# Where the first expert weights wait and in what pieces their places are filled again, in a decoder block on one core

## The chip, the cores and the metric

The kernel runs on one core of a Trainium2 chip. The metric is the device time of one execution in microseconds. Three runs of the kernel before gave 1254.2, 1250.68 and 1254.37 us, a median of 1254.2 us.

## The reference, cut to what matters

One decoder block over 256 tokens and 16 meta tokens, all float32. The first half normalises the stream, projects it, runs a pooling branch and a Mamba-2 branch, and merges them. The second half is a mixture of 64 experts in which each token uses two:

```python
def expert_block(args):
    xblk, e = args
    gu = xblk @ w_gu[e]                     # 1024 x 1024
    g, u = jnp.split(gu, 2, axis=-1)
    return (jax.nn.silu(g) * u) @ w_dn[e]   # 512 x 1024
...
y = yb * row_w[:, None].astype(yb.dtype)
out = jnp.zeros((T + 1, D), yb.dtype).at[row_tok].add(y)[:T]
```

The kernel reads the weights of all 64 experts, whatever the routing: 64 x (1024 x 1024 + 512 x 1024) x 4 bytes, which is 384 pieces of 1 MB (a MB is 1024 x 1024 bytes in this text, 1048.6 KB of the profile's GB/s).

## The kernel before, in words

**Rounds and items.** The experts go by in 16 rounds `q` of four. A round has 24 items of 1 MB, a tile of 128 x 2048 floats each: items 0 to 15 are gate and up weights, read by `up(q, xT)` at line 1094 in the order of `k` and `h`, and items 16 to 23 are down weights, read by `down` at line 1107. The items of all rounds are numbered through, so that item 24 is the first of round 1; the text calls them by these numbers (the item that the short description calls the 49th MB is 48). An item is worked on by eight matmul records on TensorE. Between `up` and `down` of a round TensorE gathers the next round's tokens (lines 978 and 969) and applies the gate (lines 993 to 1002).

**Where items lie.** Nearly all of SBUF outside the constants is one tile, `arena`, of 16 slots of 1 MB, in four blocks of four: block 0 holds the slots `r_w`, block 1 `s_rw` and `s_ce`, block 2 `s_yn` and `s_xs`, block 3 `s_bt`. During the first half it holds activations and the weights `wf`. Beside it there are `extra` (1 MB), `aux` (2 MB, used for items 11 and 12 and then for other things), rooms that the pools of the first half leave free (`mgA`, `mgB`, `ws...`), and, from the end of round 0, the tile `four` of 4 MB, which takes the place of those rooms.

**Who loads what.** Every weight load is issued by SyncE's queue (SP), in the order in which the program emits it. The first 25 items (`slots`, `load_e`, `load_1`, line 234) go one by one into places as the first half leaves them, between about 170 and 345 us. Then a load is emitted right behind the last use of the item whose place it takes: `used(m)` is called when the matmuls of item `m` have been emitted, and the load that it emits waits for them. Three kinds follow one another:

- `again` (line 261): items 25 to 39 go into places of the first 25, in pieces of one or two.
- `load_4` (line 248): from item 40, four items in one load of 4 MB, into one of five rooms (`rooms`: `four` and the blocks 3, 2, 0, 1), after the items in the list `frees`.
- line 251: the last eight items one by one.

The lists that set this are these:

```python
again = {0: (25, 1, s_xs[0]), 1: (26, 1, s_xs[1]), 4: (28, 2, two(a_bt)), ...}
frees = [23, 33, 35, 37, 39] + list(range(NS2 + 3, 16 * 24, 4))
```

An entry `m: (a, n, place)` says that after item `m` the `n` items from `a` are loaded into `place`. So in the kernel before item 23 frees the room for items 40 to 43, item 33 that for 44 to 47, item 35 that for 48 to 51, 37 and 39 those for 52 to 59, and from 43 on every fourth item frees one room.

A load on SP also waits until the eighth load before it has landed, since eight semaphores go round.

Of the kernel before, what the change touches and what calls it, by code (L numbers as in the profile page):

```python
# [9 lines left out]
FT = mybir.dt.float32  # L10
# [51 lines left out]
def block(ctx: ExitStack, tc: tile.TileContext, x, meta, csta_d, cstb_d, cstc_d, nfin_d, wf, gu_d, dn_d, out):  # L62
# [22 lines left out]
    extra = keep.tile([128, 2048], FT, name="extra")  # L85
    ACOLS = 32768
    ar = keep.tile([128, ACOLS], FT, name="arena")
# [5 lines left out]
    class Rot:  # L93
# [3 lines left out]
        def next(self):  # L97
# [6 lines left out]
    SLOT = 2048  # L104
    a_w = a
    a += NW * CHUNK
    a_row = a
# [4 lines left out]
    a_ce = a  # L112
# [6 lines left out]
    a_yn = a  # L119
# [10 lines left out]
    a_bt = a  # L130
# [30 lines left out]
    r_w = [ar[:, a_w + i * SLOT:a_w + (i + 1) * SLOT] for i in range(4)]  # L161
    s_xs, s_yn, s_rw, s_ce = [[ar[:, o + i * SLOT:o + (i + 1) * SLOT] for i in range(2)] for o in (a_xs, a_yn, a_row, a_ce)]
    s_bt = [ar[:, a_bt + i * SLOT:a_bt + (i + 1) * SLOT] for i in range(4)]
    WO0 = NSTEP - 8
    r_ws = [f"ws{(WO0 + k) % 4}" for k in range(4, 8)]
    slots = [s_xs[0], s_xs[1], s_rw[1], s_bt[0], s_bt[1], s_bt[3], s_rw[0], s_bt[2], r_w[0], s_yn[0], s_yn[1]]
    ONCE = len(slots)
    slots += [None, None, r_w[2], r_w[3], r_w[1], "mgA", r_ws[0], s_ce[0], s_ce[1], r_ws[1], "mgB", r_ws[2], r_ws[3], extra]
    NS = len(slots)
    assert NS == 25  # L170

    two = lambda o: ar[:, o:o + 2 * SLOT]
    again = {0: (25, 1, s_xs[0]), 1: (26, 1, s_xs[1]), 4: (28, 2, two(a_bt)), 6: (30, 2, two(a_row)), 7: (32, 2, two(a_bt + 2 * SLOT)),
             8: (27, 1, r_w[0]), 10: (34, 2, two(a_yn)), 14: (36, 2, two(a_w + 2 * SLOT)), 19: (38, 2, two(a_ce))}
    NS2 = NS + sum(n for _, n, _ in again.values())
    assert NS2 == 40
    slots += [None] * (NS2 - NS)
    for m_, n_, r_ in again.values():
        for j_ in range(n_):
            slots[m_ + j_] = r_[:, j_ * SLOT:(j_ + 1) * SLOT]  # L180

    rooms = [None] + [ar[:, i * 4 * SLOT:(i + 1) * 4 * SLOT] for i in (3, 2, 0, 1)]
    frees = [23, 33, 35, 37, 39] + list(range(NS2 + 3, 16 * 24, 4))

    def slot(m):
        return slots[m] if m < NS2 else part_of(rooms[(m - NS2) // 4 % 5], m % 4)
# [33 lines left out]
    n_e = [0]  # L220
    PER = 24

    def src_of(m, n=1):

        q, i = divmod(m, PER)
        v = gu_d[q, i // 4] if i < 16 else dn_d[q, (i - 16) // 4]
        return v[:, (m % 4) * SLOT:(m % 4 + n) * SLOT]

    def load_1(m):

        if isinstance(slots[m], str):
            pool = wsp if slots[m].startswith("ws") else mgp
            slots[m] = pool.tile([128, SLOT], FT, name="room" + slots[m], tag=slots[m], bufs=1)
        nc.sync.dma_start(out=slot(m), in_=src_of(m))

    def load_e():
        load_1(n_e[0])
        n_e[0] += 1

    n_4 = [NS2]  # L240
# [1 line left out]
    def load_4():  # L242
        m = n_4[0]
        n_4[0] += 4
        if m >= 16 * PER:
            return
        if m < 16 * PER - 8:
            nc.sync.dma_start(out=rooms[(m - NS2) // 4 % 5], in_=src_of(m, 4))
        else:
            for j in range(4):  # L250
                nc.sync.dma_start(out=slot(m + j), in_=src_of(m + j))

    def used(m):

        if m == 23:
            right.close()
            p = ctx.enter_context(tc.tile_pool(name="four", bufs=1, side="right", reuse_waits="tile"))
            rooms[0] = p.tile([128, 4 * SLOT], FT, name="four")
        if m in again:
            a_, n_, r_ = again[m]  # L260
            nc.sync.dma_start(out=r_, in_=src_of(a_, n_))
        if m in frees:
            load_4()
# [93 lines left out]
    for src, n, i in ((xm, NM, 2), (xh[:, 0, :], 128, 0), (xh[:, 1, :], 128, 1)):  # L357
        a_, b_ = slice(0, 512), slice(512, 1024)
# [353 lines left out]
    for n_ in (46, 46, 46, 57, 58, 68, 74, 80, 81, 82, 88):  # L712
        at(n_, load_e)
# [21 lines left out]
    n = NPROJ  # L735
# [60 lines left out]
    for k in range(8):  # L796
        wh, wl = get_piece(n)
        n += 1
        if k < 6:
            merge(k + 2)  # L800
        for _ in range((3, 0, 1, 0, 0, 0, 0, 0)[k]):
            load_e()
        W_[k] = wh, wl
        for kk, t in (((k, 0), (k, 1)), (), ((6, 0), (7, 0), (6, 1), (7, 1)))[0 if k < 6 else k - 5]:
            mh, ml = mgh[kk][:, t * 128:(t + 1) * 128], mgl[kk][:, t * 128:(t + 1) * 128]
            wh, wl = W_[kk]
            for lw, rw, f, l in ((mh, wh, True, False), (mh, wl, False, False), (ml, wh, False, True)):
                for h in range(2):
                    T.matmul(wo[2 * t + h], lw, rw[:, h * 512:(h + 1) * 512], start=kk == 0 and f, stop=kk == 7 and l,
                             skip_group_check=True)  # L810
        if k == 3:
            load_1(16)
        for _ in range((0, 0, 0, 0, 2, 3, 0, 0)[k]):
            load_e()
            if n_e[0] == 16:
                n_e[0] += 1
# [271 lines left out]
    def up(q, xT):  # L1088
        pg, pu = bank(mps, "pg", 1), bank(mps, "pu", 1)
        for k in range(8):  # L1090
            for h, ps in ((0, pg), (1, pu)):
                w = slot(q * PER + 2 * k + h)
                for e in range(4):
                    T.matmul(ps[32 * e:32 * e + 32], xT[:, k, 32 * e:32 * e + 32], w[:, e * 512:(e + 1) * 512],  # L1094
                             start=k == 0, stop=k == 7, skip_group_check=True)
                used(q * PER + 2 * k + h)
                if q == 15 and (k, h) == (5, 1):
                    keep_warm("gx", 12)
        return pg, pu

    def down(q, after):
        for hf in range(2):
            py = bank(mps, ("pg", "pu")[hf], 1)
            for c in range(4):
                w = slot(q * PER + 16 + 4 * hf + c)
                for e in range(4):
                    T.matmul(py[32 * e:32 * e + 32], hsT[:, c, 32 * e:32 * e + 32], w[:, e * 512:(e + 1) * 512],  # L1107
                             start=c == 0, stop=c == 3, skip_group_check=True)
                used(q * PER + 16 + 4 * hf + c)
                if q == 15 and (hf, c) in WARM:  # L1110
                    keep_warm("gx", WARM[hf, c])
            combine(py, hf, q == 0, q == 15)
            after(hf)
# [163 lines left out]
```

## Time and profile before

| | us |
|---|---|
| median of three runs | 1254.2 |
| the profiled execution | 1250.28 |
| its span, first to last instruction | 1248.7 |
| TensorE busy in the span | 969.6 |
| VectorE, ScalarE, GpSimd busy | 322.8, 293.2, 142.6 |
| packets of SP's queue (q1) | 459.94 MB (10^6 bytes), 88.2% of 16 DMA engines' span |

The page gives, for 40 equal slices of the span, the busy share of each engine, the granted TensorE clock, the mean busy share of the core's 16 DMA engines and what they moved. The chain of waits follows the work back from the last instruction; 43% of it is DMA and 40% TensorE. The first half of the block ends at about 340 us, round 0 at about 394 us and round 1 at about 434 us.

### The profile page before, as it was taken

How to read it: one execution, taken by the hardware profiler on the slowest of the kernel's cores; microseconds unless marked ns; L12 is line 12 of the kernel's file. 1: busy time of each engine (PE TensorE's matmuls, PEld its weight loads, DVE VectorE, ACT ScalarE, POOL GpSimd, SP SyncE). 2: the span in 40 equal slices, each digit the busy share in tenths (PEclk: the TensorE clock that was granted, in tenths of full speed). 3: DMA queues.
4: the chain of work that ended last, by engine and by line, in shares of the span. 5: the costliest groups of instructions: out<-in, count | busy, mean ns of one | idle time of the engine just before them, and what ended most of it. 6: DMA issues, size and time to landing. Idle time of an engine off the chain costs nothing.

```text
span 1248.7 us, 15306 instructions
## 1 busy us (share of the span) xinstructions
PE 969.6 (78%) x6621; PEld 542.6 (43%) x6621; DVE 322.8 (26%) x545; ACT 293.2 (23%) x561; POOL 142.6 (11%) x118
## 2 busy tenths in 40 slices
PE   9999999999988767676776657675568676776666
PEld 9999999899852312222221212131213222121222
DVE  6899987777721000000000000000000000000001
ACT  7887656633320101001010101010101001010102
POOL 2334444344100000000000000000000000000000
PEclk9999999999998978787878888797968787878889
DMA  7544447667998999999999999999999999999996
GB/s 291 185 156 168 169 171 268 254 252 270 376 403 367 419 431 428 433 436 432 431 430 435 435 430 430 434 434 431 431 433 434 433 428 435 434 431 431 432 427 253
DMA packets 27847, 462.04 MB, mean 370 GB/s; under 512 B 3112, under 2 KB 3440, under 8 KB 5504
## 3 DMA queue, kind: packets, MB, share of 16 engines
q1 hardware_dynamic: 27408, 459.94, 88.2%
q8 instruction: 53, 0.87, 0.3%
q10 hardware_dynamic: 368, 1.08, 0.2%
q14 instruction: 18, 0.15, 0.0%
HBM read 459.93 MB, written 1.08 MB: 369 GB/s over the span
## 4 chain that ended last, share of the span: by engine, by line
DMA 43%; PE 40%; DVE 9%; ACT 6%; issue 2%; POOL 0%; ACTq 0%; DVEq 0%; SPq 0%; POOLq 0%
DMA arena<-gu 32%; PE pg L1107 7%; DMA four<-gu 5%; PE gx L978 5%; PE pg L1094 4%; PE pu L1094 4%; DMA arena<-dn 3%; DVE whl L305 3%; ACT xT L969 3%; PE pj L328 2%; PE pj L322 2%; PE pj L324 2%; PE pj L323 2%; DMA four<-dn 2%; DVE arena L498 1%
## 5 line engine op out<-in xcount | busy, mean ns | idle before, releaser
L1094 PE MATMUL pg<-arena,xT 128*32 128x512 f32 x816 | 145.0, 791 | 123.0 <-DMA arena<-gu 123.0
L1008 DVE COPY aux<-tr 128x256 f32<-128x256 f32 x16 | 6.8, 424 | 687.4 <-PE tr L1007 687.4
L969 ACT ACTIVATE xT<-gx,csta 128x128 f32<-128x128 f32 x124 | 35.3, 367 | 526.5 <-PE gx L978 518.8
L1094 PE MATMUL pu<-arena,xT 128*32 128x512 f32 x824 | 134.7, 732 | 0.0
L305 DVE TENSOR_TENSOR whl<-arena,whl 128x1024 fp32r<-128x1024 f32 x79 | 115.3, 1462 | 26.4 <-ACT whl L304 25.8
L1094 PEld LDWEIGHTS pg<-arena,xT 128*32 128x32 f32 x816 | 27.1, 134 | 213.5 <-DMA arena<-gu 144.8
L322 PE MATMUL pj<-hn,whl 128*128 128x272 f32 (+1 forms) x384 | 113.6, 296 | 0.0
L324 PE MATMUL pj<-hn,whl 128*128 128x272 f32 (+1 forms) x384 | 109.7, 286 | 0.4 <-DVE whl L305 0.4
L323 PE MATMUL pj<-hn,whl 128*128 128x272 f32 (+1 forms) x384 | 109.5, 285 | 0.1
L1024 POOL TENSOR_TENSOR aux<-sel,wte 128x128 f32<-128x128 f32 x32 | 12.1, 399 | 831.1 <-DVE sel L921 786.8
L304 ACT ACTIVATE whl<-arena 128x1024 fp32r<-128x1024 f32 x86 | 90.5, 1057 | 52.0 <-PE so L324 28.9
L978 PE MATMUL gx<-sel,xh 128*128 128x128 f32 x480 | 61.5, 281 | 29.2 <-ACT xT L969 18.6
L1020 PE MATMUL acc<-aux 128*128 128x512 f32 x128 | 63.5, 618 | 24.1 <-ACT aux L1018 23.2
L1107 PE MATMUL pg<-arena,aux 128*32 128x512 f32 x400 | 69.2, 852 | 9.6 <-ACT aux L1002 7.1
L322 PEld LDWEIGHTS pj<-hn,whl 128*128 128x128 f32 x384 | 72.4, 188 | 2.5 <-issue 1.5
L323 PEld LDWEIGHTS pj<-hn,whl 128*128 128x128 f32 x384 | 72.6, 189 | 1.2 <-issue 1.2
L1094 PEld LDWEIGHTS pu<-arena,xT 128*32 128x32 f32 x824 | 32.7, 137 | 92.5 <-issue 92.5
L324 PEld LDWEIGHTS pj<-hn,whl 128*128 128x128 f32 x384 | 72.3, 188 | 0.6 <-DVE whl L305 0.6
L978 PEld LDWEIGHTS gx<-sel,xh 128*128 128x128 f32 x480 | 55.8, 192 | 36.2 <-ACT xT L969 21.4
L1094 PE MATMUL pg<-four,xT 128*32 128x512 f32 x192 | 37.2, 859 | 38.6 <-DMA four<-gu 38.6
L305 POOL TENSOR_TENSOR whl<-arena,whl 128x1024 fp32r<-128x1024 f32 x19 | 48.5, 2555 | 69.0 <-ACT whl L304 69.0
L1020 PEld LDWEIGHTS acc<-aux 128*128 128x128 f32 x128 | 21.7, 189 | 69.3 <-ACT aux L1018 52.3
(351 smaller groups left out, 1324.6 us busy)
## 6 DMA issues: line engine op xcount, KB each, us to landing
arena<-gu SPq DMA_DIRECT2D x44, 4096.0 KB, 42.4
arena<-dn SPq DMA_DIRECT2D x23, 4096.0 KB, 41.4
arena<-wf SPq DMA_DIRECT2D x48, 1024.0 KB, 5.0
four<-gu SPq DMA_DIRECT2D x12, 4096.0 KB, 42.8
four<-dn SPq DMA_DIRECT2D x5, 4096.0 KB, 38.0
arena<-gu SPq DMA_DIRECT2D x17, 1024.0 KB, 7.5
arena<-gu SPq DMA_DIRECT2D x6, 2048.0 KB, 17.7
arena<-dn SPq DMA_DIRECT2D x6, 1024.0 KB, 34.4
```

Source lines behind the costliest of these rows:

```text
L304: S.activation(wh, w, AF.Copy)
L305: (G if n in on_pool else V).tensor_tensor(out=wl, in0=w, in1=wh.bitcast(FT), op=OP.subtract)
L322: T.matmul(ps, wh, ah, start=start, stop=False, skip_group_check=True)
L323: T.matmul(ps, wh, al, start=False, stop=False, skip_group_check=True)
L324: T.matmul(ps, wl, ah, start=False, stop=stop, skip_group_check=True)
L328: T.matmul(ps.rearrange("p (i n) -> p i n", n=NT), wh, a, start=start, stop=False, skip_group_check=True)
L498: V.scalar_tensor_tensor(out=acc[:, j:], in0=ps[:, :NA - j], scalar=cs("cw", ct * 4 + 3 - j), in1=acc[:, j:], op0=OP.mult, op1=OP.add)
L969: S.activation(xT[:, 4 * b + k, :], ps[:, k * 128:(k + 1) * 128], AF.Copy, scale=cs("nf", 4 * b + k))
L978: T.matmul(ps[:, k * 128:(k + 1) * 128], xh[:, t, (4 * b + k) * 128:(4 * b + k + 1) * 128], sel[:, t, :], start=t == 0, stop=t == 1, skip_ ...
L1020: T.matmul(acc[t][h], ctv[:, t * 128:(t + 1) * 128], yv, start=first, stop=last, skip_group_check=True)
L1094: T.matmul(ps[32 * e:32 * e + 32], xT[:, k, 32 * e:32 * e + 32], w[:, e * 512:(e + 1) * 512], start=k == 0, stop=k == 7, skip_group_check= ...
L1107: T.matmul(py[32 * e:32 * e + 32], hsT[:, c, 32 * e:32 * e + 32], w[:, e * 512:(e + 1) * 512], start=c == 0, stop=c == 3, skip_group_check ...
```

## The change

The order in which the places are filled before round 0 stays, place by place (the new list `order`), but the items that lie in them change: items 0 to 3 lie in block 3, 4 to 7 in block 2, 8 and 9 in half of block 1, and 10, 13, 14 and 15 in block 0. So items that are used one behind the other share a block. The second pass (`again`) now covers items 25 to 47 instead of 25 to 39, in pieces of one to four, and rooms of 4 MB (`load_4`) begin with item 48 instead of 40.

| after item | loads, before | loads, after |
|---|---|---|
| 0 to 5 | 25; 26; 28 and 29 (after 4) | 25; 26; 27; 28; 29; 32, one each |
| 6 to 10 | 30, 31; 32, 33; 27; 34, 35 | 30, 31 (after 7); 34, 35 (after 9) |
| 14, 15 | 36, 37 (after 14) | 36 to 39 (after 15) |
| 18, 19 | 38, 39 (after 19) | 33; 40 |
| 23 | 40 to 43 | 41 to 43 |
| 24, 25, 27 | nothing | 44; 45; 46, 47 |
| 32, 33, 35, 37 | 44 to 47 (33); 48 to 51 (35); 52 to 55 (37) | 48 to 51 (32) |
| 39, 40 | 56 to 59 (39) | 52 to 55 (39); 56 to 59 (40) |
| 43, 47, ... | 60 to 63; 64 to 67; ... | the same |

```diff
-    slots = [s_xs[0], s_xs[1], s_rw[1], s_bt[0], s_bt[1], s_bt[3], s_rw[0], s_bt[2], r_w[0], s_yn[0], s_yn[1]]
+    slots = s_bt + s_xs + s_yn + s_rw + [r_w[0]]
...
+    order = [4, 5, 9, 0, 1, 3, 8, 2, 10, 6, 7] + list(range(11, 24))
...
-    again = {0: (25, 1, s_xs[0]), 1: (26, 1, s_xs[1]), 4: (28, 2, two(a_bt)), 6: (30, 2, two(a_row)), 7: (32, 2, two(a_bt + 2 * SLOT)),
-             8: (27, 1, r_w[0]), 10: (34, 2, two(a_yn)), 14: (36, 2, two(a_w + 2 * SLOT)), 19: (38, 2, two(a_ce))}
+    again = {0: (25, 1, s_bt[0]), 1: (26, 1, s_bt[1]), 2: (27, 1, s_bt[2]), 3: (28, 1, s_bt[3]), 4: (29, 1, s_xs[0]), 5: (32, 1, s_xs[1]),
+             7: (30, 2, two(a_yn)), 9: (34, 2, two(a_row)), 15: (36, 4, ar[:, a_w:a_w + 4 * SLOT]), 18: (33, 1, s_ce[0]), 19: (40, 1, s_ce[1]),
+             23: (41, 3, None), 24: (44, 1, extra), 25: (45, 1, s_bt[0]), 27: (46, 2, two(a_bt + SLOT))}
...
-    rooms = [None] + [ar[:, i * 4 * SLOT:(i + 1) * 4 * SLOT] for i in (3, 2, 0, 1)]
-    frees = [23, 33, 35, 37, 39] + list(range(NS2 + 3, 16 * 24, 4))
+    rooms = [ar[:, i * 4 * SLOT:(i + 1) * 4 * SLOT] if i < 4 else None for i in (2, 0, 1, 4, 3)]
+    frees = [32, 39, 40, 43, 47] + list(range(NS2 + 3, 16 * 24, 4))
...
     def load_e():
-        load_1(n_e[0])
+        load_1(order[n_e[0]])
         n_e[0] += 1
...
-            rooms[0] = p.tile([128, 4 * SLOT], FT, name="four")
+            rooms[3] = p.tile([128, 4 * SLOT], FT, name="four")
         if m in again:
             a_, n_, r_ = again[m]
+            if r_ is None:
+                r_ = rooms[3][:, 0:n_ * SLOT]
+                place(a_, n_, r_)
             nc.sync.dma_start(out=r_, in_=src_of(a_, n_))
```

On SP's queue the rows up to the last load of the first pass (`room<-dn`) are the same in both kernels but for line numbers. Behind it stands, in the kernel before (a row of 128x2048 is 1 MB, 128x4096 two, 128x8192 four; L261 is the second pass, L248 the rooms of 4 MB):

```order
L234 DMA room<-dn 128x2048
L261 DMA arena<-gu 128x2048 x2
L261 DMA arena<-gu 128x4096 x3
L261 DMA arena<-gu 128x2048
L261 DMA arena<-gu 128x4096 x3
L248 DMA four<-dn 128x8192
L248 DMA arena<-dn 128x8192
L248 DMA arena<-gu 128x8192 x3
L248 DMA four<-gu 128x8192
```

and in the kernel after (L272 is the second pass, L256 the rooms of 4 MB):

```order
L242 DMA room<-dn 128x2048
L272 DMA arena<-gu 128x2048 x6
L272 DMA arena<-gu 128x4096 x2
L272 DMA arena<-gu 128x8192
L272 DMA arena<-gu 128x2048
L272 DMA arena<-dn 128x2048
L272 DMA four<-dn 128x6144
L272 DMA extra<-dn 128x2048
L272 DMA arena<-dn 128x2048
L272 DMA arena<-dn 128x4096
L256 DMA arena<-gu 128x8192 x3
L256 DMA four<-gu 128x8192
```

Items 25 to 47 are carried by 15 loads instead of 11; the single load of 44 to 47 that stood behind `four<-dn` has become three loads into `extra` and two places of block 3. From item 48 on every load is one of 4 MB in both.

On TensorE the only rows that differ say where `down(1)` and the rounds behind it read their weights. Before:

```order
L999 MATMUL tr<-ident,aux 128x128 x4
L1107 MATMUL pg<-four,aux 32x512 x16
L1020 MATMUL acc_3821<-aux 128x512
L1020 MATMUL acc_3823<-aux 128x512
L1107 MATMUL pu<-arena,aux 32x512 x16
```

After:

```order
L1010 MATMUL tr<-ident,aux 128x128 x4
L1118 MATMUL pg<-arena,aux 32x512 x4
L1118 MATMUL pg<-four,aux 32x512 x12
L1031 MATMUL acc_3821<-aux 128x512
L1031 MATMUL acc_3823<-aux 128x512
L1118 MATMUL pu<-extra,aux 32x512 x4
L1118 MATMUL pu<-arena,aux 32x512 x12
```

Item 40 now lies in `arena`, items 41 to 43 in `four`, 44 in `extra` and 45 to 47 in `arena`; the number and the order of the matmuls are unchanged. The rows of VectorE, ScalarE and GpSimd are the same.

## Rows read from the trace of the kernel before

**Rows 1.** The page's 40 slices of 31.2 us each: clock, DMA share, GB/s.

```profile
PEclk9999999999998978787878888797968787878889
DMA  7544447667998999999999999999999999999996
GB/s 291 185 156 168 169 171 268 254 252 270 376 403 367 419 431 428 433 436 432 431 430 435 435 430 430 434 434 431 431 433 434 433 428 435 434 431 431 432 427 253
```

**Rows 2.** Windows by stage: bounds, length, busy per engine (count), clock, DMA share, GB/s.

```profile
core 0: us, PE busy (x) PEld busy (x) DVE busy (x) ACT busy (x) POOL busy (x), PEclk, DMA share, GB/s
352.00:356.00 4.00, 4.00 (x44) 1.24 (x40) 0.00 (x0) 3.90 (x15) 0.00 (x0) 1.00 0.78 236
356.00:392.00 36.00, 27.85 (x205) 11.65 (x198) 4.93 (x22) 6.22 (x14) 2.12 (x7) 0.91 1.03 432
392.00:400.00 8.00, 7.11 (x46) 2.95 (x48) 2.20 (x13) 0.00 (x0) 0.00 (x0) 0.79 0.94 399
400.00:410.00 10.00, 10.00 (x100) 3.09 (x96) 0.00 (x0) 0.00 (x0) 0.00 (x0) 1.00 0.52 195
410.00:450.00 40.00, 26.62 (x202) 10.47 (x194) 1.73 (x5) 4.65 (x12) 0.76 (x2) 0.96 1.01 434
450.00:1180.00 730.00, 500.53 (x3054) 171.36 (x3050) 22.52 (x65) 60.53 (x156) 9.87 (x26) 0.82 1.00 432
1230.00:1238.00 8.00, 6.86 (x48) 2.79 (x49) 1.38 (x2) 1.37 (x4) 0.00 (x0) 1.00 0.46 189
```

**Rows 3.** SP's queue in order of time, 378 to 445 us: start, length, line, load.

```profile
383.80 0.33 SPq L261 DMA_DIRECT2D arena<-gu  x1
390.07 0.33 SPq L248 DMA_DIRECT2D four<-dn  x1
405.79 0.33 SPq L248 DMA_DIRECT2D arena<-dn  x1
407.51 3.76 SPq L248 DMA_DIRECT2D arena<-gu  x3
424.94 0.33 SPq L248 DMA_DIRECT2D four<-gu  x1
431.27 6.66 SPq L248 DMA_DIRECT2D arena<-dn  x2
```

**Rows 4.** Windows of 2 us from 400 to 408 us, columns as in rows 2.

```profile
400.00:402.00 2.00, 2.00 (x24) 0.62 (x20) 0.00 (x0) 0.00 (x0) 0.00 (x0) 1.00 0.68 270
402.00:404.00 2.00, 2.00 (x24) 0.65 (x20) 0.00 (x0) 0.00 (x0) 0.00 (x0) 1.00 0.15 66
404.00:406.00 2.00, 2.00 (x26) 0.54 (x20) 0.00 (x0) 0.00 (x0) 0.00 (x0) 1.00 0.00 0
406.00:408.00 2.00, 2.00 (x24) 0.63 (x20) 0.00 (x0) 0.00 (x0) 0.00 (x0) 1.00 0.91 262
```

**Rows 5.** Chain of waits, 394 to 462 us: start, length, what ended last.

```profile
395.31 1.84 PE pg L1094 x8
397.15 1.71 PE pu L1094 x8
398.86 0.86 PE pg L1094 x8
399.72 0.86 PE pu L1094 x8
...
404.01 0.86 PE pg L1094 x8
404.87 0.86 PE pu L1094 x8
...
410.02 0.86 PE pu L1094 x8
...
421.24 3.69 PE pg L1107 x32
...
424.94 33.05 DMA four<-gu
```

**Rows 6.** Loads issued at 364.6, 390.1 and 405.8 us: count, KB, us to landing.

```profile
arena<-gu SPq DMA_DIRECT2D x1, 2048.0 KB, 23.9
...
four<-dn SPq DMA_DIRECT2D x1, 4096.0 KB, 15.1
...
arena<-dn SPq DMA_DIRECT2D x1, 4096.0 KB, 12.1
```

**Rows 7.** A stretch of loads of 1 MB alone, columns as in rows 2.

```profile
340.00:350.00 10.00, 10.00 (x87) 9.62 (x86) 7.08 (x37) 2.93 (x8) 0.00 (x0) 1.00 1.01 423
```

**Rows 8.** Chain of waits at the end, from 1175 us.

```profile
1175.54 6.08 PE pg L1107 x32
...
1181.64 35.74 DMA arena<-gu
...
1217.44 20.05 DMA four<-dn
...
1237.54 1.11 PE pu L1107 x8
```

More of the change, by code (lines that the diff above doesn't have):

```diff
@@ L170, in block, with place @@
     assert NS == 25
+    order = [4, 5, 9, 0, 1, 3, 8, 2, 10, 6, 7] + list(range(11, 24))
     two = lambda o: ar[:, o:o + 2 * SLOT]
-    again = {0: (25, 1, s_xs[0]), 1: (26, 1, s_xs[1]), 4: (28, 2, two(a_bt)), 6: (30, 2, two(a_row)), 7: (32, 2, two(a_bt + 2 * SLOT)),
-             8: (27, 1, r_w[0]), 10: (34, 2, two(a_yn)), 14: (36, 2, two(a_w + 2 * SLOT)), 19: (38, 2, two(a_ce))}
+    again = {0: (25, 1, s_bt[0]), 1: (26, 1, s_bt[1]), 2: (27, 1, s_bt[2]), 3: (28, 1, s_bt[3]), 4: (29, 1, s_xs[0]), 5: (32, 1, s_xs[1]),
+             7: (30, 2, two(a_yn)), 9: (34, 2, two(a_row)), 15: (36, 4, ar[:, a_w:a_w + 4 * SLOT]), 18: (33, 1, s_ce[0]), 19: (40, 1, s_ce[1]),
+             23: (41, 3, None), 24: (44, 1, extra), 25: (45, 1, s_bt[0]), 27: (46, 2, two(a_bt + SLOT))}
     NS2 = NS + sum(n for _, n, _ in again.values())
-    assert NS2 == 40
+    assert NS2 == 48
     slots += [None] * (NS2 - NS)
+    def place(m, n, r):
+        for j in range(n):
+            slots[m + j] = r[:, j * SLOT:(j + 1) * SLOT]
     for m_, n_, r_ in again.values():
-        for j_ in range(n_):
-            slots[m_ + j_] = r_[:, j_ * SLOT:(j_ + 1) * SLOT]
-    rooms = [None] + [ar[:, i * 4 * SLOT:(i + 1) * 4 * SLOT] for i in (3, 2, 0, 1)]
-    frees = [23, 33, 35, 37, 39] + list(range(NS2 + 3, 16 * 24, 4))
+        if r_ is not None:
+            place(m_, n_, r_)
+    rooms = [ar[:, i * 4 * SLOT:(i + 1) * 4 * SLOT] if i < 4 else None for i in (2, 0, 1, 4, 3)]
+    frees = [32, 39, 40, 43, 47] + list(range(NS2 + 3, 16 * 24, 4))
     def slot(m):
```

## The prediction

> **What bounds the kernel now.** I read the page's slices first [rows 1]. From the eleventh slice on, that is from about 320 us, the 16 DMA engines are busy all the time at about 432 GB/s, with one slice below its neighbours: the thirteenth, 375 to 406 us, with 367 GB/s. Behind it TensorE's clock falls again and again, because TensorE waits. The windows by stage make this exact [rows 2]: from 450 to 1180 us the share is 1.00 at 432 GB/s while TensorE works in 500.53 of 730 us. The rounds are bound by the weights' transfer, and TensorE has room for some 30% more. So the end comes when the last weight has landed, and only two things move it: the bytes, which the change leaves alone, and the time in which the DMA engines have nothing to carry.
>
> The same windows show that time. From 352 to 356 us there are 236 GB/s, from 392 to 400 us 399, from 400 to 410 us only 195, and both neighbours of that stretch run at 432 and 434. SP's queue tells why [rows 3]: after the load at 390.07 us (items 40 to 43) the next one leaves at 405.79 us. In the windows of 2 us the share is 0.68, 0.15 and 0.00 before it, and 0.91 after it [rows 4]. What the load at 405.79 waits for stands in the chain of waits [rows 5]: round 1's `up` starts at 395.31 us, its first two items take 1.84 and 1.71 us and the others 0.86, and its tenth item, item 33, ends at 404.87 + 0.86 = 405.73 us. Item 33 is what frees the room for 44 to 47. TensorE is at work all the time there; the queue is empty because no room is free by the kernel's lists. Further on the chain is a wait for a load of 4 MB, 33.05 us long, and so it goes to the end [rows 5, 8].
>
> **The change, part by part.** *The first items.* The places are filled at the same times and in the same order; only which item lies in each changes. The last of these loads leave before 350 us, and until then the first half sets the pace. The items that come later in the new order of places (6 and 7 instead of 9 and 10) are loaded well before `up(0)`, which starts at about 350 us. I cost this at nothing; what hides it is the first half's work on TensorE, which is busy for 10.00 of 10 us from 340 to 350 [rows 7].
>
> *The second pass up to item 23.* Items 0 to 5 free one place each instead of 0, 1 and 4. The first two loads leave as before, so the dip at 352 to 356 us stays. By item 19, 16 MB are out instead of 15. Before, the 15th MB was nearly carried when `four<-dn` left at 390.07: the share of 392 to 400 us, 399 GB/s against 432, is worth 8 x 33 / 432 = 0.6 us. One MB takes 1.0486 / 432 = 2.43 us, so the 16th keeps the engines busy until about 394 us and I expect this to go too.
>
> *Items 44 to 47.* This is the core. Nineteen MB are out by 390 us in both kernels and are carried by about 401 to 402 us [rows 4]. In the new lists item 24 releases 44, item 25 releases 45 and item 27 releases 46 and 47: by the chain these leave at 397.15, 398.86 and about 400.6 us [rows 5]. The first of them is more than 4 us ahead of the empty queue, and the load into the empty queue at 405.79 was moving bytes within the next window [rows 4], so 4 us are enough. Four more MB last 9.7 us, until about 411. Item 32 (ends at 404.87) releases 48 to 51, which last until 421; item 39 (ends at 410.88) releases 52 to 55, until 431; item 40, the first of `down(1)`, ends at 421.24 + 3.69 / 4 = 422.2 and releases 56 to 59; and 60 to 63 leave at 424.94 as before. Each release stands 9 us or more ahead of the moment at which the queue would run dry. Nothing is late next: what was a hole is filled through to the steady rounds, whose lists are the same.
>
> *New waits.* Item 33 now stands behind 36 to 39 in the queue. It is the 15th MB, so it lands by about 393 us and is read at 404.87. The new loads wait for the eighth load before them; with pieces of 1 MB that one is some 10 MB older and has landed. Four more loads on SP cost four issues of 0.33 us each [rows 3] on a queue that sits idle for tens of us: nothing.
>
> *The size of the hole.* Over all 16 engines it is (432 - 195) / 432 x 10 = 5.5 us from 400 to 410, and with the 0.6 us above 6.1 us: the upper end. But a load has landed only when its slowest engine is through. The load at 364.6 us landed at 364.6 + 23.9 = 388.5, that of 390.07 at 405.2, that of 405.79 at 417.9 [rows 6]. From 388.5 to 417.9 there landed 2 + 4 + 4 = 10 MB, 24.3 us of work in 29.4 us: 5.1 us lost for the last engine. From 405.2 to 417.9 alone it is 12.7 - 9.7 = 3.0 us, the lower end, if the engine that lagged at 405 would have lagged on. I take 5.1, since it is measured on landings over the whole hole.
>
> *Smaller pieces.* Ten loads of 1 MB take the place of three. In a stretch of 1-MB loads alone the engines move 423 GB/s [rows 7], which is 2.48 instead of 2.43 us per MB: 7 x 0.05 = 0.4 us lost. [...]
>
> **Sum.** 5.1 - 0.4 = 4.7 us. Against the profiled execution (span 1248.7, with 1.58 us around it 1250.28) that is 1245.6 us. This execution and one of the three runs lie 3.5 to 3.9 us below the median of 1254.2; from the median the same sum gives 1249.5 us, which I predict.
>
> **Rivals.**
>
> *The slowest DMA engine sets the gain.* The engines do not finish together: at the end, where the queue runs dry, the share over 1230 to 1238 us is only 0.46, and at 402 to 404 it is 0.15 while the load that it belongs to lands at 405.2 [rows 2, 4, 6]. In the kernel before, the hole lets an engine that lags catch up, since all start again together; with the hole filled, the lag of 3 us at 405 stays and adds to what gathers until 1237. Then the gain is 3.0 - 0.4 = 2.6 us and the time 1251.6. For it speaks the slope of the drain; against it, that the lag need not fall on the engines that are last at the end.
>
> *Starts that add up: slower.* A load that comes into an empty queue took 12.1 us for what takes 9.7 in a full one [rows 6]: 2.4 us of start. If the four additional loads each paid it, 9.6 us would be lost and 5.1 won, 1254.2 + 4.5 = 1258.7 us. It decides as soon as the queue holds nothing behind the load in work, which could happen between 397 and 405 us if `up(1)` started later than now. Against it stand the 423 GB/s of the 1-MB loads [rows 7] and the lead of 4 us. [...]
>
> *The hole only moves: no change.* Were `up(1)` to wait for item 33, or `down(1)` for 40, the later rooms would come free later, and the same 5 us would lie between 411 and 425 us: 1254.2. The margins of 9 us above speak against it.
>
> **How the numbers follow.** The forecast has a chance of 0.70, the slowest engine 0.16, the hole that moves 0.08, the added starts 0.06. A measurement of this kernel can tell about 0.3%, 3.8 us, from no change. The forecast lies only 0.9 us beyond that, and runs of the same kernel lie up to 3.7 us apart, so of its 0.70 I count 0.58 as faster and 0.12 as the same. The slowest engine gives 0.04 faster, 0.11 same, 0.01 slower; the hole that moves 0.07 same and 0.01 slower; the added starts 0.01 same and 0.05 slower. Together 0.62 faster, 0.31 same, 0.07 slower. The range begins at the upper end of the hole taken from the faster runs, 1250.28 - 6.1 = 1244.2, and reaches to no gain at all, 1254.5; the forecast's own range is 1244.2 to 1251.6.
>
> **What would show it.** In the changed kernel's profile: loads on SP at about 397, 399 and 400.6 us; a DMA share near 1.00 and over 420 GB/s in every window between 392 and 450 us; the load of 60 to 63 landing near 453 us instead of 458; the same 432 GB/s from 450 us on; the last weight landing some 5 us before 1237.5 us and the same 11 us from there to the end [rows 8]. A share below 0.9 between 405 and 430 us would mean that the hole has moved; a full share there with less than 3 us won at the end, that the slowest engine sets it; and a lower rate in the stretch of small loads, that starts add up. A different rate in the steady rounds would prove the whole sum wrong, since 730 us at 432 GB/s weigh far more than the hole.

## The result, and the profile after

| | before | after |
|---|---|---|
| median of the first measurement (5 runs each), us | 1254.14 | 1243.56 |
| its ratio, with the 95% interval | | 0.9939 [0.9921, 0.9956] |
| median of a later session on one chip (29 and 6 runs), us | 1250.46 | 1243.60 |
| its ratio | | 0.9952 [0.9936, 0.9968] |
| the profiled execution, us | 1250.28 | 1243.56 |

The kernel became faster. The forecast was 1249.5 us with a range from 1244.2 to 1254.5; the time lies 0.6 us below that range. Three of the five runs of before in the first measurement lie between 1254.1 and 1254.4 us; of the 81 runs of before in the three sessions below 8 lie near 1254 (1253.9 to 1254.6), and the others between 1246.9 and 1252.1. So the first ratio flatters the change: the gain is 6.7 us from execution to execution and 6.9 us between the medians of the later session.

First the page's slices of the kernel after, as in [rows 1]:

```profile
PEclk9999999999999987887888878887888887878789
DMA  7544447677999999999999999999999999999996
GB/s 292 185 157 170 170 170 272 242 266 268 361 408 427 442 427 434 435 426 436 434 428 436 430 432 435 429 433 432 433 432 429 437 432 430 435 432 432 435 423 253
```

The thirteenth slice now has 427 GB/s instead of 367, and from there on none falls below 423 but the last. The windows by stage, columns as in [rows 2]:

```profile
352.00:356.00 4.00, 4.00 (x44) 1.27 (x40) 0.27 (x2) 3.69 (x13) 0.00 (x0) 1.00 0.83 276
356.00:392.00 36.00, 27.85 (x209) 11.77 (x198) 4.67 (x21) 6.04 (x13) 2.12 (x7) 0.95 1.01 427
392.00:400.00 8.00, 7.12 (x66) 2.93 (x69) 2.20 (x13) 0.00 (x0) 0.00 (x0) 1.00 1.03 443
400.00:410.00 10.00, 9.29 (x88) 3.13 (x77) 0.82 (x3) 0.00 (x0) 0.62 (x2) 1.00 1.00 424
410.00:450.00 40.00, 29.21 (x204) 10.44 (x203) 0.91 (x2) 4.65 (x12) 0.14 (x1) 0.91 1.01 435
450.00:1180.00 730.00, 502.66 (x3046) 171.91 (x3050) 22.54 (x65) 61.13 (x157) 9.86 (x26) 0.82 1.00 433
1230.00:1238.00 8.00, 3.59 (x17) 1.18 (x16) 2.17 (x5) 3.60 (x8) 0.00 (x0) 0.96 0.03 14
```

The hole is gone: 424 GB/s from 400 to 410 us where there were 195, and 443 from 392 to 400 where there were 399. The neighbours and the 730 us of steady rounds are as before. In the last window there is almost nothing left to carry (14 GB/s), where before the share was still 0.46: the drain has moved forward.

SP's queue, as in [rows 3]. The row of three at 402.25 stands for loads at 402.25 (items 48 to 51), 408.26 and 420.55 us, that of two at 396.24 for 396.24 (item 45) and 397.96 (46, 47):

```profile
389.09 0.33 SPq L272 DMA_DIRECT2D four<-dn  x1
395.39 0.33 SPq L272 DMA_DIRECT2D extra<-dn  x1
396.24 2.04 SPq L272 DMA_DIRECT2D arena<-dn  x2
402.25 18.62 SPq L256 DMA_DIRECT2D arena<-gu  x3
423.72 0.33 SPq L256 DMA_DIRECT2D four<-gu  x1
430.05 6.66 SPq L256 DMA_DIRECT2D arena<-dn  x2
```

The gap of 15.7 us in the queue has become gaps of at most 12.3 us, and each lies behind loads of 4 MB that are still being carried. The chain of waits, as in [rows 5]:

```profile
394.33 1.00 PE pg L1105 x8
395.32 0.86 PE pu L1105 x8
396.18 0.86 PE pg L1105 x8
397.04 0.86 PE pu L1105 x8
...
418.55 5.15 PE pg L1118 x32
423.72 28.15 DMA four<-gu
451.92 1.66 PE pg L1105 x8
```

Item 24 ends at 395.32 us and its load leaves at 395.39; item 27 ends at 397.90, and 46 and 47 leave at 397.96. The load of 60 to 63 leaves 1.2 us earlier than before and lands 6.1 us earlier, at 451.9. The end of the chain, as in [rows 8]:

```profile
1176.67 34.63 DMA arena<-gu
...
1211.36 19.70 DMA four<-dn
...
1231.10 1.11 PE pu L1118 x8
```

The last weight is there at 1231.1 us instead of 1237.5, 6.4 us earlier.

### The profile page after: what moved, and what is told of

It reads as the page before. It is cut to its first block, busy times and chain, and to the rows that moved or that the text cites. A ratio compares the mean times of both kernels' runs of the same rounds, so it can differ in the third digit from the quotient of the medians.

```text
span 1242.0 us, 15313 instructions
## 1 busy us (share of the span) xinstructions
PE 970.4 (78%) x6621; PEld 542.1 (44%) x6621; DVE 322.7 (26%) x545; ACT 293.1 (24%) x561; POOL 142.6 (11%) x118
## 4 chain that ended last, share of the span: by engine, by line
DMA 43%; PE 39%; DVE 9%; ACT 6%; issue 2%; POOL 0%; DVEq 0%; ACTq 0%; SPq 0%; POOLq 0%
DMA arena<-gu 32%; PE pg L1118 7%; DMA four<-gu 5%; PE gx L989 5%; PE pg L1105 4%; PE pu L1105 4%; DMA arena<-dn 3%; DVE whl L316 3%; ACT xT L980 3%; PE pj L339 2%; PE pj L333 2%; PE pj L335 2%; PE pj L334 2%; DMA four<-dn 2%; DVE arena L509 1%
## 5 line engine op out<-in xcount | busy, mean ns | idle before, releaser
L1118 PE MATMUL pg<-arena,aux 128*32 128x512 f32 x408 | 71.7, 862 | 9.4 <-ACT aux L1013 7.8
```

## The experiments

Eleven programs ran, in three sessions with their own runs of before (medians 1250.11, 1250.46 and 1249.68 us); e1 and e9 are the two kernels unchanged. Diffs are against the kernel named; in them `again` entries read "after item: (first item, number, place)". The question was twofold: is it the hole of 400 to 410 us that pays, and what made it wider or narrower from run to run?

**e1, before once more.** No edit.

> The kernel before once more, unchanged, for the spread of its runs and a second trace. Its runs lie in two groups, near 1250.7 and near 1254.2 us. Theory (the hole is as long as TensorE takes to come to item 33): the mean granted clock listed for each run falls as its time rises by some 3 to 4 us, and the second trace shows the load of items 44 to 47 leaving at a time that differs from 405.8 us by the difference of the two executions' times. Rival (the groups come from something else, a rate or the first half): the load leaves within 1 us of 405.8 us whatever the time.

Measured: 1249.51 us, ratio 1.0 [0.9986, 1.0014]. In this execution the granted clock was 1.00 (2.4 GHz) when `up(1)` began, from 395 to 398 us, where the profile of before has 0.50 (1.2 GHz) from 396 to 398; in both TensorE had just waited twice for VectorE, for less than 1 us each time. The first two items, and the load that ends the hole:

```profile
395.60 1.00 PE pg L1094 x8
396.60 0.86 PE pu L1094 x8
```

```profile
404.38 0.33 SPq L248 DMA_DIRECT2D arena<-dn  x1
```

Before, the same two items took 1.84 and 1.71 us [rows 5]. The load of 44 to 47 left at 404.38 us instead of 405.79, and the execution took 1248.61 instead of 1250.28 us: 1.4 us here, 1.7 there. That is the first hint that the moment of this one load sets the time of before. The expected account of the two groups failed: the three runs near 1254 us have mean clocks of 0.884 to 0.893, the others 0.880 to 0.896, so the clock does not fall as the time rises.

**e2, the late rooms as one load, emitted behind item 33 (against after).**

```diff
-             23: (41, 3, None), 24: (44, 1, extra), 25: (45, 1, s_bt[0]), 27: (46, 2, two(a_bt + SLOT))}
+             23: (41, 3, None), 33: (44, 4, ar[:, a_bt:a_bt + 4 * SLOT])}
...
-    frees = [32, 39, 40, 43, 47] + list(range(NS2 + 3, 16 * 24, 4))
+    frees = [35, 39, 40, 43, 47] + list(range(NS2 + 3, 16 * 24, 4))
```

> The changed kernel with its late pieces undone: items 44 to 47 in one load after item 33 as before (into block 3), items 48 to 51 after item 35; the new layout and the finer pieces up to item 23 stay. Theory (the gain is the hole at 400 to 410 us): the hole is back, of 4 to 6 us, and 1248 to 1251 us, within 2 us of the kernel before's faster runs. Rival (the gain is in the layout, or in the pieces up to item 23): 1244 us, as the changed kernel.

Measured: 1245.46 us, ratio 0.9959 [0.9945, 0.9974]. The hole did not come back, since the load did not wait for item 33. It left at 400.23 us, behind the last reader of its place, item 28, which ended at 400.17; item 33 ended at 404.46. The load, and item 28 in the chain:

```profile
400.23 0.33 SPq L272 DMA_DIRECT2D arena<-dn  x1
```

```profile
399.31 0.86 PE pg L1105 x8
```

The edit moved the load in the program, not on the chip, and 364 GB/s remain from 400 to 410 us. My expectation was built on the wrong wait; e8 does what e2 was meant to do.

**e3, the late rooms as one load behind item 28 (against after).**

```diff
-             23: (41, 3, None), 24: (44, 1, extra), 25: (45, 1, s_bt[0]), 27: (46, 2, two(a_bt + SLOT))}
+             23: (41, 3, None), 28: (44, 4, ar[:, a_bt:a_bt + 4 * SLOT])}
```

> The changed kernel with items 44 to 47 in one load of 4 MB after item 28 (into block 3), in place of three loads after 24, 25 and 27; the load leaves at about 399 us, still ahead of the empty queue. Theory (only the moment counts, not the pieces): 1243.6 us within 1 us. Rival (small pieces cost a start of 2 us each): 4 us faster, near 1239.6. Rival (the early lead of 397 us is needed): 2 us or more slower, and a share well below 1 around 402 us.

Measured: 1245.68 us, ratio 0.9967 [0.9954, 0.9981], some 2 us more than after in another session, with intervals that overlap. The load left at 400.47 us and not at the expected 399, since the first two items ran at half the clock here (1.77 and 1.71 us); the queue had only a little left (a share of 0.23 from 400 to 401 us), and 378 GB/s remain in the ten microseconds. Whatever one load in place of three may save, it does not outweigh leaving 2 to 5 us later.

**e8, the late rooms as one load that truly waits for item 32's place (against after).** Item 32 is the last reader of block 2 here; items 48 to 51 take block 3 in exchange.

```diff
-             23: (41, 3, None), 24: (44, 1, extra), 25: (45, 1, s_bt[0]), 27: (46, 2, two(a_bt + SLOT))}
+             23: (41, 3, None), 32: (44, 4, ar[:, a_yn:a_yn + 4 * SLOT])}
...
-    rooms = [ar[:, i * 4 * SLOT:(i + 1) * 4 * SLOT] if i < 4 else None for i in (2, 0, 1, 4, 3)]
-    frees = [32, 39, 40, 43, 47] + list(range(NS2 + 3, 16 * 24, 4))
+    rooms = [ar[:, i * 4 * SLOT:(i + 1) * 4 * SLOT] if i < 4 else None for i in (3, 0, 1, 4, 2)]
+    frees = [33, 39, 40, 43, 47] + list(range(NS2 + 3, 16 * 24, 4))
```

> The changed kernel with items 44 to 47 in one load into block 2, which is free only when item 32 has been read, and items 48 to 51 in block 3 in its stead; the new layout and the pieces up to item 23 stay. (In the run with the load emitted after item 33 it left at 400.2 us, since its place, block 3, was free after item 28: a load waits for the last reader of its place, not for the item behind which it is emitted.) Theory (the gain is the moment at which 44 leaves): the load leaves at about 404 us, the hole is back, and the run is 3.5 to 5 us slower than the changed kernel. Rival (the gain is in the pieces up to item 23): within 1 us of the changed kernel.

Measured: 1248.57 us, ratio 0.9985 [0.9973, 0.9997]. Its load of 44 to 47 and the window of the hole:

```profile
402.68 0.33 SPq L272 DMA_DIRECT2D arena<-dn  x1
```

```profile
400.00:410.00 10.00, 9.29 (x88) 2.83 (x77) 0.82 (x3) 0.00 (x0) 0.20 (x1) 1.00 0.72 281
```

With the rest of the change in place, the later place of these four items brings the hole back, and 5.0 of the 6.9 us are lost (1248.57 against 1243.60 in the same session).

**e10, the late pieces alone, with the old layout and the old second pass (against before).** Cut to its core:

```diff
-             8: (27, 1, r_w[0]), 10: (34, 2, two(a_yn)), 14: (36, 2, two(a_w + 2 * SLOT)), 19: (38, 2, two(a_ce))}
+             8: (27, 1, r_w[0]), 10: (34, 2, two(a_yn)), 14: (36, 2, two(a_w + 2 * SLOT)), 19: (38, 2, two(a_ce)),
+             23: (40, 4, None), 24: (44, 1, extra), 25: (45, 1, s_xs[0]), 26: (46, 1, s_xs[1]), 27: (47, 1, r_w[0])}
...
+    rooms = [ar[:, i * 4 * SLOT:(i + 1) * 4 * SLOT] if i < 4 else None for i in (3, 1, 4, 2, 0)]
+    frees = [33, 39, 43, 46, 47] + list(range(NS2 + 3, 16 * 24, 4))
```

> The late pieces alone, on the layout and the second pass of the kernel before: items 44 to 47 leave one by one after items 24 to 27 (into extra and the three places of 25, 26 and 27), and the rooms of 4 MB follow from item 48 after items 33, 39, 43, 46 and 47. Theory (all that counts is that a load leaves before the queue is empty): nearly the whole gain, 0.995 to 0.996 of the kernel before, within 1 us of the changed kernel; 0.6 us may be lost at 392 us, where the load after item 23 still follows an almost empty queue. Rival (the new layout and the pieces up to item 23 carry part of the gain): 2 us or more slower than the changed kernel.

Measured: 1245.5 us, ratio 0.9966 [0.9954, 0.9978]: 4.2 us of gain in its session. That is 1.9 us above the median of after (another session) and 1.4 above that of e12, which is after with a small addition, in the same session, so neither the theory (within 1 us) nor the rival (2 us or more) came out, and the intervals of e10 and e12 overlap. Its windows:

```profile
392.00:400.00 8.00, 7.12 (x43) 3.11 (x45) 2.21 (x13) 0.00 (x0) 0.00 (x0) 0.79 0.96 401
400.00:410.00 10.00, 10.00 (x96) 2.99 (x92) 0.00 (x0) 0.00 (x0) 0.00 (x0) 1.00 0.96 405
```

The first keeps its 401 GB/s (399 in before [rows 2]), since one MB less is out when `four<-dn` leaves; against after that is (443 - 401) x 8 / 432 = 0.8 us, and the second row adds (424 - 405) x 10 / 432 = 0.4. So e8 and e10 divide the gain from both sides: the pieces 44 to 47 carry most of it, 4 to 5 us, and 1 to 2 us are left for the rest of the change. Of these the second pass up to item 23 is shown to carry the 0.8 us of the first window. The profiled execution of e10 lies 2.7 us above that of after; 1.2 us of this are in the two windows, and 1.4 us stand at the very end, where the last piece took 21.15 us to land instead of 19.70; whether that belongs to the edit, which also changes the order of the rooms, is not shown. The layout of the first items alone was not tried; it is what makes the places come free in this order.

**e4, one MB of the four early (against before).** Item 44 goes into `extra` behind item 24; 45 to 47 wait as before.

```diff
     def slot(m):
+        if m == 44:
+            return extra
...
-        if m < 16 * PER - 8:
+        if m == 44:
+            nc.sync.dma_start(out=rooms[1][:, SLOT:4 * SLOT], in_=src_of(45, 3))
+        elif m < 16 * PER - 8:
...
+        if m == 24:
+            nc.sync.dma_start(out=extra, in_=src_of(44))
```

> The kernel before with one edit: item 44 goes into the free 1 MB of extra after item 24, and 45 to 47 follow after item 33. Theory (each MB put ahead of item 33 fills 2.43 us of the hole): 2.4 us faster than the kernel before, ratio about 0.998, and DMA busy some 2.4 us longer between 400 and 410 us. Rival (the slowest DMA engine sets the end, so that a hole filled by half gives nothing, or the layout matters): no change, ratio 1.000.

Measured: 1247.8 us, ratio 0.9981 [0.9968, 0.9994], 2.3 us of gain. One MB at 432 GB/s is 2.43 us: one MB in the hole is worth about its own time.

**e5 and e6, 24 idle matmuls ahead of `up(1)`, in before and in after.** They delay what releases the rooms and touch no load.

```diff
     for q in range(16):
+        if q == 1:
+            keep_warm("gx", 24)
         pg, pu = up(q, xT)
```

> The kernel before with 24 additional matmuls of 128x128 on TensorE (into a bank that nothing reads then) ahead of round 1's first item, about 6 us of TensorE's time. Theory (the hole ends when TensorE comes to item 33): the whole run is as much slower as the matmuls take, about 6 us, though TensorE is idle for a third of every later round. Rival (the rounds have room for TensorE, so a delay of 6 us is hidden): less than 1 us slower.

> The changed kernel with the same 24 additional matmuls. Theory (item 44 leaves 5 to 6 us ahead of the empty queue): nearly all of the 6 us is hidden, 0 to 2 us slower than the changed kernel, and 10 us or more faster than the kernel before with the same matmuls. Rival (both are bound by TensorE in round 1): 6 us slower than the changed kernel.

Measured: before with the delay 1253.98 us, ratio 1.0032 [1.0021, 1.0042]; after with it 1245.43 us, ratio 0.9967 [0.9954, 0.998]. In e5 the matmuls took 5.36 us and `up(1)` began at 401.03 us:

```profile
395.67 5.36 PE gx L936 x48
401.03 1.00 PE pg L1094 x8
402.03 0.86 PE pu L1094 x8
```

But its first items then ran at the full clock, so that the load of 44 to 47 left at 409.81, 4.0 us later than in the profile of before, and the execution took 1254.04, 3.8 us more. Against e1, which had the full clock too, the load left 5.43 us later and the execution took 5.43 us more, which is the length of the matmuls (5.36): the matmuls cost their own length, as expected, where executions with the same clock are compared, while the medians differ by 3.5 us. In after the same delay costs 1.8 us: item 44 left at 401.01 us, with the queue nearly empty, and 400 to 410 us shows 333 GB/s. After with the matmuls is 8.6 us faster than before with them, not the expected 10: of the 3.5 us that the delay costs before at the median, after swallows half.

**e7 and e12, 2 x 8 idle matmuls inside the list building ahead of `up(1)`, to keep the clock up, in before and in after.**

```diff
+        keep_warm("gx", 8)
         ov = mt([128, 8], "ov")
...
+        keep_warm("gx", 8)
         V.tensor_scalar(out=ov[:, 4:5], in0=ps[:, 0:1], scalar1=1.0, scalar2=None, op0=OP.add)
```

> The kernel before with twice 8 matmuls of 128x128 on TensorE in its gaps between round 0 and round 1, to keep its granted clock up while it waits for VectorE there. In the traces so far in which the queue runs empty, the profiled time is the moment L at which the first load into the empty queue leaves plus 844.2 us, within 0.3 us. Theory (TensorE's pace to item 33 sets the end, so its clock counts although the rounds are bound by DMA): no item of round 1 takes longer than 1 us, L between 403.5 and 405.5 us, the profiled time L + 844.2, and the median 1 to 2 us below the kernel before's. Rival (the clock does not matter): the median within 0.5 us.

> The changed kernel with the same matmuls in the gaps. Theory (no load waits for TensorE while the queue is empty): the median within 0.7 us of the changed kernel's 1243.6. Rival (a higher clock in round 1 helps both kernels): 1 to 2 us faster.

Measured: e7 1251.34 us, ratio 1.0009 [0.9997, 1.0021]; e12 1244.12 us, ratio 0.9952 [0.9938, 0.9966]. The expectation of e7 failed. The matmuls did not lie beside the wait, they stood in the chain:

```profile
394.12 0.34 PE tr L1060 x4
394.46 1.89 PE gx L936 x16
...
396.69 1.89 PE gx L936 x16
398.59 0.45 PE tr L1082 x4
399.03 1.00 PE pg L1096 x8
400.03 0.86 PE pu L1096 x8
```

They won the clock (1.00 and 0.86 us for the first two items) but `up(1)` began 3.7 us later than in the profile of before. Of these 1.35 us were there already ahead of the matmuls (the row of line 1060, `PE tr L1060 x4`, starts at 394.12 us against 392.77 in before), and 2.4 us came between it and `up(1)`, 4.91 us against 2.54. So the matmuls cost 2.4 us and won 1.7. The expected median, 1 to 2 us below before, became one 1.7 us above it. The row of line 1060 in before:

```profile
392.77 0.35 PE tr L1060 x4
```

In after the same edit gives 1244.12 us, within the expected 0.7 us of the 1243.6 of after in another session. Its window of the hole:

```profile
400.00:410.00 10.00, 10.00 (x100) 2.99 (x93) 0.00 (x0) 0.00 (x0) 0.00 (x0) 1.00 0.98 378
```

Item 44 left at 398.40 us, 3.0 us later than in after. In e2, e3 and e6, where nothing followed the load of 41 to 43 by then, the share falls to 0.18 to 0.24 from 400 to 401 us, so the lead was some 2 us here. The engines were busy all the time and moved fewer bytes, which is worth 10 x 54 / 432 = 1.2 us. It is the one sign of a loss when small pieces meet a nearly empty queue; that the pieces are its cause was not tested.

**e9, after once more.** No edit.

> The changed kernel once more, unchanged, beside the others on one chip. Theory (the hole of 392 to 412 us, and nothing else, is filled): 0.994 to 0.995 of the kernel before, with no window below 420 GB/s between 392 and 450 us. Rival (part of the first 0.9939 was the runs of before near 1254 us): 0.996 or above.

Measured: 1243.6 us, ratio 0.9952 [0.9936, 0.9968], just above the 0.994 to 0.995 expected. This execution had the low clock at the start of `up(1)`, first its chain, then its windows:

```profile
394.16 1.76 PE pg L1105 x8
395.92 1.71 PE pu L1105 x8
```

```profile
392.00:400.00 8.00, 7.16 (x48) 2.70 (x52) 2.20 (x13) 0.00 (x0) 0.00 (x0) 0.79 1.01 434
400.00:410.00 10.00, 10.00 (x94) 2.93 (x86) 0.00 (x0) 0.00 (x0) 0.00 (x0) 1.00 1.06 451
```

The queue is full all the same, and the execution took 1242.16 us. The high clock of the first profile of after was not what paid.

**What the runs say together.** In the profiled executions in which the queue runs empty, the time hangs on one moment, when the load that ends the hole leaves:

| kernel | load of 44 to 47 leaves, us | execution, us | difference |
|---|---|---|---|
| e2 | 400.23 | 1244.52 | 844.3 |
| e3 | 400.47 | 1244.70 | 844.2 |
| e8 | 402.68 | 1246.85 | 844.2 |
| e1 | 404.38 | 1248.61 | 844.2 |
| before | 405.79 | 1250.28 | 844.5 |
| e7 | 407.81 | 1252.03 | 844.2 |
| e5 | 409.81 | 1254.04 | 844.2 |
| e6 (44 alone, then the others) | 401.01 | 1244.86 | 843.9 |
| e4 (45 to 47 alone) | 405.23 | 1246.78 | 841.6 |

In the first seven rows, over 9.6 us of that moment, the rest of the program is constant to 0.3 us; e6 lies 0.3 us below them, and in e4, where one of the four MB is already out, it is 2.6 us shorter. The rest is 340 MB of 2.43 us, 825 us, and 19 us of start, drain and last work. After, e9 and e12 take less than any line of the table; their queue does not run empty there. Nor does that of e10 (the lowest share in one microsecond is 0.54), which takes 1246.22 us though item 44 leaves at 397.43.

## Why the prediction was right, and where its size was not

The mechanism came out as forecast, the size did not. Of the 5.9 us by which 1249.5 us missed, 3.9 are the base from which the sum was taken and 2.0 the sum itself. The two steps that failed are that base and, inside the sum, the size of the hole.

**What bounds the kernel: right.** The steady rounds kept 433 GB/s, the tail from the last weight on 12.5 us (12.7 before), and the empty queue moved the time; the table above shows it more strictly than the one trace could. One reading was off: the eleventh and twelfth slice have 376 and 403 GB/s and not 432 [rows 1]. They changed little (361 and 408 after), and nothing in the sum rests on them.

**The releases: right.** Forecast 397.15, 398.86 and about 400.6 us; measured 395.39, 396.24 and 397.96. `up(1)` began 1.0 us earlier than in the profile of before, and the first two items at full clock give 0.8 and 1.7 us more. In e9, with the low clock, item 44 left at 395.96 us and no hole came either, so some 4 us of lead suffice. They are not generous: with 2 us (e12) 378 GB/s are left in the window, and with one load at 400.47 us (e3) or three from 401.01 us (e6) the median is some 2 us higher. The margins of 9 us that the prediction gives for the later releases do not follow from its own figures: 48 to 51 at 404.87 us against 411 is 6 us, 56 to 59 at 422.2 against 431 is 8.8. They were enough all the same: 48 to 51 left at 402.25 us, 56 to 59 at 420.55.

**Landing of 60 to 63: right.** Forecast near 453 us, measured 451.9.

**The size of the hole: too small; this is the step of the sum that failed.** I took 5.1 us from the landings of the last engine, and 6.1 from all 16 engines as the upper end. From the windows of both kernels the engines moved more by (276 - 236) x 4 / 432 = 0.4 us from 352 to 356, 0.4 us less from 356 to 392, 0.8 us more from 392 to 400, 5.3 us from 400 to 410 and 0.1 to 450: 6.1 us together. The last weight came 6.4 us earlier. So the engines' lag at 405 us was hardly carried on to the end, and in this pair of executions the mean over all engines was the right measure of an empty stretch.

**The small pieces: no loss found in a filled queue.** I charged 0.4 us for 1-MB loads. From 392 to 400 us the queue of after, with pieces of 1 to 3 MB in it, ran at 443 GB/s. From 356 to 392 us, behind six loads of 1 MB, the seven kernels with the new second pass (after, e2, e3, e6, e8, e9, e12) ran at 427 to 429 GB/s, the six with the old one at 417 to 432. For 44 to 47 alone e3, with one load instead of three, is not the faster one, but its load also left later.

**The sum.** 1243.56 against a forecast of 1245.6 from the profiled execution: 2.0 us too little gain, of which 1.0 is the hole, 0.4 the pieces, 0.3 the shorter tail. The remaining 0.3 us is about the lead in bytes that after already had at 352 us (82.75 against 82.58 MB on SP's queue, 0.4 us); it comes from the first half, and one execution of each can't tell it from chance. The base: I carried the sum to a median of three runs, two of which lay near 1254 us, though the profiled execution stood at 1250.28. Whether it was chance that three of the first five runs lay there, against 8 of 81 later, is not known; it made the first ratio larger than the later ones. Why about one run of before in ten takes some 4 us more stays open; the clock at the start of `up(1)` explains 1 to 2 us, not 4, and no profile fell on such a run. It does not take the hole: e3 to e9 have one or two such runs each, 3.4 to 6.1 us above the median, and e9 among them (1246.98 us) is after itself.

**The rivals.** The slowest engine sets the gain (1251.6): refuted, 6.7 us were won where it gives 2.6. Starts that add up (1258.7): refuted by the rates above and by the time itself. A load into the empty queue did take 2.4 us more than in a full one [rows 6], but four more loads into a queue that was not empty show none of the 9.6 us that this would have added. The Trainium skill, "DMA: Bandwidth & Descriptors", section "Anatomy of one DMA — SWDGE (gpsimd) path", gives a fixed cost of about 2 us for a transfer that GpSimd issues. The loads here are issued by SyncE, and for them the runs show the 2.4 us of a load into an empty queue and nothing for each load in a filled one. The hole only moves (1254.2): refuted, 435 GB/s from 410 to 450 us. One late place is enough for a hole, as e8 shows: the whole change has 281 GB/s from 400 to 410 us when the place for 44 to 47 comes free 7 us later than that of the first small piece.

## What to carry to other kernels

When transfers bound a kernel, look for the windows in which the DMA share falls below its steady value, and value each one as the missing bytes over the steady rate, on the mean of all engines (6.1 us here, where the last weight came 6.4 us earlier). Then find the load that ends the hole and the last reader of the place that it fills: what must change is which place comes free when, and a load written elsewhere in the program behind the same reader moves nothing. Before carrying a sum of a few microseconds to a median, ask whether the median and the profiled execution belong to the same runs.

## What the runs showed of the hardware that I had not expected

- TensorE's clock reaches the time of this transfer-bound kernel through the empty queue. In before, two items at 1.84 and 1.71 us delay the one load that counts; in e1, at 1.00 and 0.86 us, it left 1.4 us earlier. In e9 two such slow items cost nothing, with 434 and 451 GB/s around them.
- A stretch of matmuls meant to hold the clock up has its own price on the chain: two sets of 8 in e7, 1.89 us each, made the way to `up(1)` 2.4 us longer, more than the 1.7 us that the two slow items lose.
